# One fixed expert instead of two, its down projection at once, and expert weights in 16 KB rows

## The chip, the cores and the metric

The kernel runs on one core of one Trainium2 chip. The metric is the device time of one execution in microseconds (us). A time of the profiled execution is told beside the span that its profile covers, from the first to the last instruction. MB here is 2^20 bytes, as in the sizes of the transfers; GB/s are 10^9 bytes a second, as the profile prints them.

## The reference, cut to what matters

One decoder layer on 256 tokens of width 1024, all in float32. First a token mixer (layer norm, one wide input projection, two causal convolutions, gates, output projection), then a mixture of 32 experts, of which each token takes its four best:

```python
    logits = (xf @ router_w + router_b).astype(jnp.float32)
    top_v, top_i = lax.top_k(logits, TOP_K)          # TOP_K = 4 of 32
    gate = jax.nn.softmax(top_v, axis=-1).astype(u.dtype)
    ...
    def expert_block(args):
        xb, e = args
        h = clamped_swiglu(xb @ w1[e] + b1[e])       # w1[e]: 1024 x 2048
        return h @ w2[e] + b2[e]                     # w2[e]: 1024 x 1024
    ...
    y = jax.ops.segment_sum(ys * row_w[:, None], row_tok, num_segments=n_tok)
```

An expert has 8 MB of w1 and 4 MB of w2, so 384 MB of weights go through the second half. The routing of the reference, evaluated on its inputs, gives the experts between 0 and 136 tokens each; expert 0 has 26, expert 1 none, and it is the only one with none.

## The kernel before

**Two halves.** The mixer streams its weights (w_in, w_pb, w_pa, w_o and the modulation weights ada_w) as 64 transfers of 1 MB through a pool of sixteen 1 MB buffers, `wpool`. The expert half streams 384 transfers of 1 MB. Every weight transfer is issued by SP, in program order.

**Experts.** Tokens are gathered per expert in units of 32 (`gather`, a product of three bf16 parts of the normalised tokens with a selection matrix), go through w1 (`up`, accumulating over eight k-tiles of 128 rows), are transposed and put through the activation (`copy_up` on ACT, `turn` on TensorE, `swiglu` on VectorE), and through w2 (`down`). Four units make a group, and `combine` multiplies their gated rows back to the tokens. `ROOM[e]` is the number of units that the program reserves for the e-th expert in its order.

**Order.** The first `FIXED` = 2 experts are number 0 and 1, whatever the routing. The other 30 are taken in an order worked out on the chip: `rank()` counts for each expert how many have more tokens, and `plan_` says which rank stands at which place of the order (a 5-unit place for the largest, the last place for the smallest). `ordered()` turns the ranks with two products into `oc`, the numbers and token counts of the experts in their order. SP reads `oc` into registers before it issues the loads of an expert.

**Loads.** `order` lists the chunks: the eight of w1 of expert e, then the four of w2 of expert e-1. A w1 chunk is 128 rows of 8 KB; a w2 chunk is 256 rows of 4 KB, two for each partition. A ring of 17 buffers (the sixteen of `wpool` and one more) holds them. The first 17 loads are issued without a condition; every later one is issued by `used(e, k)`, in the program's place where the chunk 17 earlier has had its last product:

```python
            t = wtile()
            nc.sync.dma_start(t.rearrange("p (k f) -> p k f", k=src.shape[1]), src, cond=None if always else tokens > 0)
```

So a load whose expert has no token moves nothing.

**The expert loop.** For each e: `up(e)`, the gather of expert e+2, `down(e-1)`, the activation of e, and `combine` for finished groups. Small steps are put between the k-tiles of the first two `up`s as hooks: for expert 0 `ordered`, `in_order` of the positions, `bias1`, the gather of expert 1 and `in_order` of the gates; for expert 1 `select_gates(0)`, `gain` (the output gate as a row) and `bias2` (the gated second bias, added to the residual).

**The branch.** After expert 29, `beyond()` tests whether any expert has more tokens than its room, and if so works those off in loops; with these inputs it has none. At the end of that branch SP waits for all transfers in flight (the eight semaphores of its queue) before it goes on, and ACT waits for SP.

Of the kernel before, what the change touches and what calls it, by code (L numbers as in the profile page):

```python
# [20 lines left out]
SEQ = 256  # L21
KT = D // 128
NT = SEQ // 128
NE = 32
# [9 lines left out]

WBUFS = 16
XBUFS = 1
RING = WBUFS + XBUFS
NUNIT = SEQ // 32
# [72 lines left out]
def mixer_moe_kernel(ctx, tc, x, cond, packed, ada_w, ada_g1, w_in, w_pa, w_pb, w_o, ln1, ln2, router_b, w1, b1, w2, b2, plan, out):  # L111
    nc = tc.nc
    ctx.enter_context(tc.manual_schedule())
    wpool = ctx.enter_context(tc.tile_pool(name="wpool", bufs=WBUFS))
    keep = ctx.enter_context(tc.tile_pool(name="keep", bufs=1))
    state = {"pools": [wpool] * WBUFS, "n": 0, "ring": None}

    def wtile():
        pools, n = state["pools"], state["n"]
        state["n"] += 1  # L120
        ring = state["ring"]
        if ring is not None and n >= len(pools):
            return ring[n % len(pools)]
        t = pools[n % len(pools)].tile([128, 2048], F32, name="wchunk")
        if ring is not None:
            ring.append(t)
        return t

# [130 lines left out]

    xstack = ctx.enter_context(ExitStack())  # L260
    with ExitStack() as p1:
# [365 lines left out]
        wstack.close()  # L627
        xpool = xstack.enter_context(tc.tile_pool(name="xpool", bufs=XBUFS, side="right", reuse_waits="tile"))
        late = p1.enter_context(tc.tile_pool(name="late", bufs=1, reuse_waits="tile"))
# [159 lines left out]
    with ExitStack() as p2:  # L789
        one = p2.enter_context(tc.tile_pool(name="one", bufs=1, reuse_waits="tile"))  # L790
        sm = p2.enter_context(tc.tile_pool(name="sm2", bufs=1, reuse_waits="tile"))
        psb = p2.enter_context(tc.tile_pool(name="psb", bufs=1, space=PSUM, reuse_waits="tile"))
        state["pools"] = [wpool] * (WBUFS - 4) + [xpool] * XBUFS + [wpool] * 4
        state["n"] = 0
        state["ring"] = []
        ph = [psb.tile([128, 512], F32, name=f"ph{i}") for i in range(5)]
# [55 lines left out]
        def locate(e):  # L852

            if e < FIXED:
                where[e] = e, value(counts[0:1, e:e + 1], SEQ, (ENG.SP,))
            elif e < NE:
                where[e] = tuple(value(oc[0:1, v, e:e + 1], (NE - 1, SEQ)[v], (ENG.SP,)) for v in range(2))

        def load(n):
            if n >= len(order):  # L860
                return
            e, k = order[n]
            always = n < RING
            if k == 0 and e >= FIXED:
                if e == FIXED:
                    locate(e)
                locate(e + 1)
            if not always and e not in where:
                locate(e)
            i, tokens = where[e] if not always else (e, None)  # L870
            if k < KT:
                src = w1[bass.ds(i, 1), k * 128:(k + 1) * 128, :].rearrange("a p f -> p a f")
            else:
                src = w2[bass.ds(i, 1), (k - KT) * 256:(k - KT + 1) * 256, :].rearrange("a (k p) f -> p (a k) f", p=128)
            t = wtile()
            nc.sync.dma_start(t.rearrange("p (k f) -> p k f", k=src.shape[1]), src, cond=None if always else tokens > 0)  # L876
            wt[e, k] = t

        def used(e, k):
# [46 lines left out]
        def up(e, hooks={}):  # L926
            xt = xt_of(e)
            for kt in range(KT):
                w = wt[e, kt]
# [34 lines left out]
        def down(e):  # L964
            ddg = ddg_of(e)
            for u in range(ROOM[e]):
                q = bank_of[e, u]
                y, yt_, ys, cm = py[q % 2], yt[q % 2], ys_[:, q // 4 % 2, :], cms[q // 4 % 2]
                r = slice(32 * (q % 4), 32 * (q % 4) + 32)
                turn_gates(y, r, ddg[:, :, u * SLOT:(u + 1) * SLOT])  # L970
                for kt in range(KT):
                    o = (kt % 2) * 1024
                    w = wt[e, KT + kt // 2]
                    down_mm(y, acts[:, u], kt, [w[:, o + g * 256:o + (g + 1) * 256] for g in range(4)])
# [8 lines left out]
        def combine(i, banks, add=True):  # L983
            for t in range(NT):
                for h in range(2):
                    b = banks[(2 * t + h) % len(banks)]
                    nc.tensor.matmul(b, cms[i % 2][:, t * 128:(t + 1) * 128], ys_[:, i % 2, h * 512:h * 512 + 512],  # L987
                                     start=True, stop=True)
# [52 lines left out]
        def bias2():  # L1041
            for h in range(2):
                for t in range(NT):
                    a = X[:, t, h * 512:(h + 1) * 512]
                    nc.tensor.matmul(py[t], gatesT[:, t, :], b2w[0:NE, h * 512:(h + 1) * 512], start=True, stop=True)
                    tmp = sm.tile([128, 512], F32, name="hb")
                    nc.vector.tensor_tensor(tmp, py[t], hss[h], op=ALU.mult)
                    nc.vector.scalar_tensor_tensor(a, a, ALPHA, tmp, op0=ALU.mult, op1=ALU.add)

        def gain():  # L1050
            ada2_out(spare, sm, 5, None, ms=ms5)
            for h in range(2):
                pb = px.rearrange("p (k c) -> p k c", k=4)
                for k in range(4):
                    c = 40 + 4 * h + k
                    nc.tensor.matmul(pb[:, k, :], modT[:, c:c + 1].to_broadcast([128, 128]), identf, start=True, stop=True)
                nc.scalar.copy(hss[h], px)
                for g in (2 * h, 2 * h + 1):
                    nc.vector.tensor_copy(g2g[32 * g:32 * g + 32, :], hss[h][32 * g:32 * g + 32, (g % 2) * 256:(g % 2) * 256 + 256])
# [10 lines left out]
        def one_beyond(j, u):  # L1070
# [16 lines left out]
            for kt in range(KT):  # L1087
                for g in range(4):
                    w = hss[g % 2]
                    nc.sync.dma_start(w[:, None, :], w1[bass.ds(e, 1), kt * 128:(kt + 1) * 128, g * 512:(g + 1) * 512]  # L1090
                                      .rearrange("a p f -> p a f"))
                    nc.tensor.matmul(p[32 * g:32 * g + 32, :], xt[:, kt], w, start=(kt == 0), stop=(kt == KT - 1),
# [6 lines left out]
            for kt in range(KT):  # L1099
                for h in range(2):  # L1100
                    w = hss[h]
                    nc.sync.dma_start(w[:, None, :], w2[bass.ds(e, 1), kt * 128:(kt + 1) * 128, h * 512:(h + 1) * 512]
                                      .rearrange("a p f -> p a f"))
                    for g in (2 * h, 2 * h + 1):
# [38 lines left out]

        def gather_1():
            for piece in gather(1, py[0]):
                piece()

        hooks = {0: {2: ordered,
                     3: lambda: in_order(posm, posT, posS, px),
                     4: bias1,  # L1150
                     5: gather_1,
                     6: lambda: in_order(gates, gatesT, gateS, px)},
                 1: {1: lambda: select_gates(0), 2: gain, 5: bias2}}
        n_combined = 0
        for e in range(NE):
            pieces = []
            up(e, hooks.get(e, {}))
            if e + 2 < NE:
                select(e + 2)
                pieces = gather(e + 2)  # L1160
            if e:
                select_gates(e)
# [4 lines left out]
            if e:  # L1167
                down(e - 1)
# [54 lines left out]


def _cols(v):
    return v.reshape(-1, 128).T
# [51 lines left out]
```

## Time and profile before

| what | value |
|---|---|
| three runs, median (lowest to highest) | 1321.57 us (1320.34 to 1322.01) |
| profiled execution, its own time | 1321.0 us |
| its span | 1319.3 us |
| PE busy | 1139.7 us (86% of the span), 11387 instructions |
| VectorE, ACT busy | 527.3 us (40%), 132.2 us (10%) |
| moved by DMA | 473.42 MB, mean 359 GB/s (10^6 bytes) |
| granted TensorE clock, mean | 0.933 |

A busy PE in this table includes matmuls that wait in the pipeline, so its 86% is not a measure of work. The span has a mixer part up to about 330 us, in which TensorE is busy throughout, a router part up to about 341 us, and the expert loop, which ends at about 1301 us; the rest is the last layer norm and the output.

### The profile page before, as it was taken

The page shows a single profiled execution, that of the slowest core. Times are in us where ns is not written, and L with a number is a line of the kernel's source. Part 1 is how long each engine was busy: PE and PEld are TensorE (multiplying, and loading weights), DVE is VectorE, ACT ScalarE, POOL GpSimd, SP SyncE. Part 2 cuts the span into 40 slices and gives each one's busy share as a digit, 9 for nine tenths or more (in the row PEclk, how much of TensorE's full clock was granted, in tenths as well). Part 3 has the DMA queues.
Part 4 walks back from the last instruction along what each step waited for, and adds up shares of the span by engine and source line. Part 5 has one row for each costly group of instructions (what it writes and reads, how often), then busy time and mean ns, then how long its engine had stood idle before and what let it go on. Part 6 is the DMA issues. An engine that isn't in the chain of part 4 may idle for free. (4 is left out here: it accounts for less than half of the span.)

```text
span 1319.3 us, 26597 instructions
## 1 busy us (share of the span) xinstructions
PE 1139.7 (86%) x11387; PEld 633.0 (48%) x11388; DVE 527.3 (40%) x1352; ACT 132.2 (10%) x288; POOL 16.8 (1%) x34
## 2 busy tenths in 40 slices
PE   5999999997899998999897899797979787786644
PEld 4888888886435433544442335333423333232211
DVE  2588753656445314441442233223322332322214
ACT  2110001102110001010100010000000000000001
POOL 0000000001000000000000000000000000000000
PEclk9999999998889998999898999998979899897777
DMA  9974644776749999999999999999999999999975
GB/s 375 421 300 156 259 153 137 285 298 243 271 181 366 416 416 416 417 415 417 416 415 416 416 416 416 416 417 416 417 416 416 416 415 412 416 416 413 413 313 204
DMA packets 82223, 473.42 MB, mean 359 GB/s; under 512 B 7633, under 2 KB 7665, under 8 KB 41106
## 3 DMA queue, kind: packets, MB, share of 16 engines
q1 hardware_dynamic: 81250, 469.03, 88.4%
q10 hardware_dynamic: 848, 2.62, 0.5%
q8 instruction: 91, 1.49, 0.5%
q14 instruction: 34, 0.28, 0.1%
HBM read 474.76 MB, written 1.05 MB: 361 GB/s over the span
## 5 line engine op out<-in xcount | busy, mean ns | idle before, releaser
L923 PE MATMUL ph<-wchunk,xt 128*32 128x512 f32 x2368 | 295.7, 642 | 45.6 <-DMA wchunk<-in_w_dram 37.9
L956 PE MATMUL py<-wchunk,acts 128*32 128x256 f32 x3584 | 242.3, 404 | 48.4 <-DMA wchunk<-in_w_dram 46.3
L582 PE MATMUL zps<-slot,wchunk 128*128 128x256 f32 x1024 | 222.3, 379 | 1.6 <-DVE slot L301 1.6
L582 PEld LDWEIGHTS zps<-slot,wchunk 128*128 128x128 f32 x1024 | 194.3, 190 | 28.9 <-DVE slot L301 1.8
L956 PEld LDWEIGHTS py<-wchunk,acts 128*32 128x32 f32 x3584 | 137.9, 115 | 125.1 <-DMA wchunk<-in_w_dram 65.8
L923 PEld LDWEIGHTS ph<-wchunk,xt 128*32 128x32 f32 x2368 | 71.5, 114 | 248.3 <-issue 146.6
L923 PE MATMUL ph<-wchunk,xtm 128*32 128x512 f32 x1216 | 131.5, 592 | 0.0
L904 DVE TENSOR_TENSOR xt<-px,modT 128x256 f32<-128x256 f32 (+1 forms) x26 | 13.4, 517 | 294.6 <-PE px L901 294.6
L977 DVE TENSOR_TENSOR yt<-py,g2g 128x256 f32<-128x256 f32 x56 | 23.8, 425 | 240.7 <-PE py L956 240.7
L316 DVE SCALAR_TENSOR_TENSOR slot<-slot,pk,slot 128x256 f32<-128x256 f32 x240 | 97.6, 480 | 2.1 <-ACT slot L312 2.1
L923 PEld LDWEIGHTS ph<-wchunk,xtm 128*32 128x32 f32 x1216 | 39.0, 110 | 90.6 <-issue 90.0
L1122 ACT COPY hs<-ph 128x512 f32<-128x512 f32 x56 | 32.7, 584 | 424.5 <-PE ph L923 391.0
L901 PEld LDWEIGHTS <-slot 128*128 128x128 bf16 x1824 | 53.6, 99 | 33.2 <-issue 33.2
L980 DVE COPY slot<-yt 32x256 f32<-32x256 f32 x224 | 63.8, 285 | 4.6
L940 PE MATMUL ph<-identf,hs 128*128 128x128 f32 x224 | 36.5, 301 | 20.8 <-ACT hs L1122 20.8
L978 ACT COPY cm<-py 32x256 f32<-32x256 f32 x56 | 20.3, 363 | 322.6 <-DVE yt L977 322.6
L987 PE MATMUL px<-slot,cm 128*128 128x512 f32 x52 | 30.9, 678 | 21.4 <-DVE slot L991 19.4
L946 DVE TENSOR_TENSOR hb<-ph,b1S 128x512 f32<-128x512 f32 x56 | 38.7, 691 | 14.8 <-PE ph L940 11.5
L940 PEld LDWEIGHTS ph<-identf,hs 128*128 128x128 f32 x224 | 26.1, 151 | 34.9 <-ACT hs L1122 23.4
L901 PE MATMUL px<-dd,slot 128*128 128x32 bf16 (+1 forms) x1248 | 38.8, 185 | 0.0
L949 ACT ACTIVATE sg<-hb 128x256 f32<-128x256 f32 x56 | 23.3, 416 | 110.8 <-DVE hb L947 110.8
L904 DVE TENSOR_TENSOR xtm<-px,modT 128x512 f32<-128x512 f32 (+1 forms) x11 | 6.8, 618 | 62.2 <-PE px L901 62.1
(245 smaller groups left out, 697.8 us busy)
## 6 DMA issues: line engine op xcount, KB each, us to landing
wchunk<-in_w_dram SPq DMA_DIRECT2D x384, 1024.0 KB, 19.9
wchunk<-in_w_in_dram SPq DMA_DIRECT2D x28, 1024.0 KB, 13.5
wchunk<-in_ada_w_dram SPq DMA_DIRECT2D x24, 1024.0 KB, 8.3
wchunk<-in_w_pb_dram SPq DMA_DIRECT2D x4, 1024.0 KB, 8.0
wchunk<-in_w_pa_dram SPq DMA_DIRECT2D x4, 1024.0 KB, 4.8
wchunk<-in_w_o_dram SPq DMA_DIRECT2D x4, 1024.0 KB, 5.0
slot<-in_x_dram SPq DMA_DIRECT2D x2, 512.0 KB
slot<-in_x_dram ACTq DMA_DIRECT2D x1, 1024.0 KB, 10.0
```

What stands on the lines that cost most here:

```text
L316: nc.vector.scalar_tensor_tensor(cv[:, b, :], ya[:, b, k:k + SEQ], par("conv_a_w", b * CONV_A + k), cv[:, b, :], op0=ALU.mult, op1=ALU.add)
L582: nc.tensor.matmul(ps, w[:, o:o + 128], rhs[:, kt, :], start=(kt == 0), stop=(kt == KT - 1))
L901: nc.tensor.matmul(pv[:, kt], npart[c][:, t, kt * 128:(kt + 1) * 128], dd[:, t], start=(t == 0 and c == 0), stop=(t == 1 and c == 2))
L923: nc.tensor.matmul(p[32 * g:32 * g + 32, :], x_, w[g], start=(kt == 0), stop=(kt == KT - 1), skip_group_check=True)
L940: nc.tensor.transpose(pt[:, f].rearrange("p g s -> p (g s)"), hs[:, f * 128:(f + 1) * 128], identf)
L946: nc.vector.tensor_tensor(hb, pt, b1v.to_broadcast([128, 4, 4, SLOT]), op=ALU.add)
L949: nc.scalar.activation(sg, glu, AF.Sigmoid, scale=SW_ALPHA)
L956: nc.tensor.matmul(y[32 * g:32 * g + 32, 0:256], act[:, kt % 4, kt // 4, :], w[g], start=(kt == 0), stop=(kt == KT - 1), skip_group_check= ...
L977: nc.vector.tensor_tensor(yt_, y[:, 0:256], g2g, op=ALU.mult)
L980: nc.vector.tensor_copy(ys[r, g * 256:(g + 1) * 256], yt_[32 * g:32 * g + 32, :])
L987: nc.tensor.matmul(b, cms[i % 2][:, t * 128:(t + 1) * 128], ys_[:, i % 2, h * 512:h * 512 + 512], start=True, stop=True)
L1122: nc.scalar.copy(hss[q % 2], ph[q % 5])
```

## The change

It does six things.

1. `FIXED` is 1: only expert 0 is fixed; expert 1 is ranked with the others. Expert 0 keeps room for two units, the added ranked place has one.
2. `ordered()` runs before the first product of `up(0)`, and `rank()` before the first gather. The six loads of expert 0 are issued ahead, all others after `oc` is known.
3. `down(0)` follows the activation of expert 0, ahead of `up(1)`; for the later experts `down(e-1)` stays where it was.
4. The host lays w1 out as four blocks and w2 as two blocks of 128 rows of 16 KB for each expert. A load is 2 MB; an expert has six. The ring has 8 buffers of 2 MB. In the mixer the same buffers are used in halves of 1 MB, so one comes free when both halves have.
5. The last expert's w2 is loaded in eight pieces of 512 KB.
6. `gain` moves into `up(0)`, `bias2` into `up(2)`; b2 is multiplied by the output gate once (32 rows), which takes four VectorE operations out of `bias2`; `combine` uses only the rows that the last group has.

```diff
-WBUFS = 16
-XBUFS = 1
-RING = WBUFS + XBUFS
+RING = 8
...
-FIXED = 2
-ROOM = [2, 2] + [int(c) for c in "121511241121412131213121212111"]
-_RANK_ROOM = [5, 4, 4, 3, 3] + [2] * 8 + [1] * 17
+FIXED = 1
+ROOM = [2] + [int(c) for c in "1121511241121412131213121212111"]
+_RANK_ROOM = [5, 4, 4, 3, 3] + [2] * 8 + [1] * 18
...
     def wtile():
...
+        if not halves_:
+            t = wpool.tile([128, 4096], F32, name="wchunk")
+            halves_.extend((t[:, 0:2048], t[:, 2048:4096]))
+        return halves_.pop(0)
...
         for e in range(NE):
-            order += [(e, k) for k in range(KT)]
-            if e:
-                order += [(e - 1, k) for k in range(KT, 12)]
-        order += [(NE - 1, k) for k in range(KT, 12)]
+            order += [(e, k) for k in range(4)]
+            if e == 0 or e > 1:
+                order += [(max(0, e - 1), k) for k in (4, 5)]
+        order += [(NE - 1, k) for k in (4, 5)]
...
-            always = n < RING
+            always = e < FIXED
...
-            t = wtile()
-            nc.sync.dma_start(t.rearrange("p (k f) -> p k f", k=src.shape[1]), src, cond=None if always else tokens > 0)
+            src = w1[bass.ds(i, 1), k:k + 1] if k < 4 else w2[bass.ds(i, 1), k - 4:k - 3]
+            src = src.rearrange("a b p f -> p (a b) f")
+            t = ring[n % RING]
+            step = 4096 if e < NE - 1 or k < 4 else 1024
+            for f in range(0, 4096, step):
+                nc.sync.dma_start(t[:, None, f:f + step], src[:, :, f:f + step], cond=None if n < RING else tokens > 0)
...
-                used(e, kt)
+                if kt % 2:
+                    used(e, kt // 2)
...
-                    if u == ROOM[e] - 1 and kt % 2:
-                        used(e, KT + kt // 2)
+                    if u == ROOM[e] - 1 and kt % 4 == 3:
+                        used(e, 4 + kt // 4)
...
-        for n in range(RING):
+        for n in range(6 * FIXED):
             load(n)
...
+        rank()
         for piece in gather(0):
             piece()
-        rank()
-        select(1)
+        ordered()
+        for n in range(6 * FIXED, RING):
+            load(n)
         softmax(sm)
...
-        hooks = {0: {2: ordered,
-                     3: lambda: in_order(posm, posT, posS, px),
-                     4: bias1,
-                     5: gather_1,
-                     6: lambda: in_order(gates, gatesT, gateS, px)},
-                 1: {1: lambda: select_gates(0), 2: gain, 5: bias2}}
+        hooks = {0: {0: lambda: in_order(posm, posT, posS, px),
+                     2: bias1,
+                     3: lambda: in_order(gates, gatesT, gateS, px),
+                     4: gather_1,
+                     6: gain},
+                 2: {3: bias2}}
...
-            if e:
+            if e > 1:
                 down(e - 1)
...
+            if e == 0:
+                down(0)
...
-        "w1": a["w1"][0],
+        "w1": _rows(a["w1"][0], 2),
...
-        "w2": a["w2"][0],
+        "w2": _rows(a["w2"][0], 4),
```

How the instructions move is seen at three places. First the loads on SP around the reading of `oc` (TENSOR_LOAD); each conditional load is an ISA instruction and a DMA. Before:

```order
L876 DMA wchunk<-in_w_dram 128x2048 x16
L876 DMA wchunk<-in_w_dram 128x2x1024
L1136 DMA slot_96<-in_b_dram 32x2048
L1137 DMA xtm<-in_b_dram 32x1024
L849 TENSOR_LOAD counts
L876 ISA
L876 DMA wchunk<-in_w_dram 128x2x1024
L876 ISA
L876 DMA wchunk<-in_w_dram 128x2x1024
L876 ISA
L876 DMA wchunk<-in_w_dram 128x2x1024
L849 TENSOR_LOAD oc x4
```

And of the change:

```order
L861 DMA wchunk<-in_w_dram 128x4096 x6
L1130 DMA slot_96<-in_b_dram 32x2048
L1131 DMA xtm<-in_b_dram 32x1024
L838 TENSOR_LOAD oc x4
L861 ISA
L861 DMA wchunk<-in_w_dram 128x4096
L861 ISA
L861 DMA wchunk<-in_w_dram 128x4096
```

Twenty loads of 1 MB stood ahead of the reading of `oc`; now six of 2 MB do, and everything behind them waits for `oc`.

Second, VectorE between the ranks (`kr`) and `oc`. Before, the softmax of the gates stands between them, and the two operations that finish the gathered tokens of expert 0 stand ahead of both:

```order
L1004 SCALAR_TENSOR_TENSOR kr<-plan__89,rk 32x32
L888 TENSOR_SCALAR dd_1993<-slot_id,posm 128x64 x2
L776 TENSOR_SCALAR dl<-lg,m_0_93 128x32
L776 TENSOR_SCALAR dl<-lg,m_1_94 128x32
L779 TENSOR_SCALAR dl<-esg 128x64
L780 TENSOR_TENSOR esg<-esg,sel 128x64
L781 RECIPROCAL dl<-dl 128x64
L782 TENSOR_TENSOR esg<-esg,dl 128x64
L784 TENSOR_REDUCE ssum<-esg 128x2
L785 RECIPROCAL ssum<-ssum 128x2
L786 TENSOR_TENSOR gates<-esg,ssum 128x64
L1010 CAST oc<-py_1986 128x64
```

And of the change:

```order
L996 SCALAR_TENSOR_TENSOR kr<-plan__89,rk 32x32
L895 TENSOR_TENSOR xt_1962<-px,modT 128x512
L895 TENSOR_TENSOR xt_1962<-xt_1962,modT 128x512
L1002 CAST oc<-py_1959 128x64
L1004 COPY tokens<-py_1959 1x32
```

`oc` now comes directly behind the gathered tokens.

Third, TensorE after `up(0)`. `ph` is the result of `up`, `py` that of `down`. Before, the transposes of expert 0 are followed by `up(1)` with its hooks, and `down(0)` comes after that:

```order
L940 MATMUL ph_1981<-identf,hs_1999 128x128 x4
L940 MATMUL ph_1982<-identf,hs_2000 128x128 x4
L923 MATMUL ph_1983<-wchunk,xt_1990 32x512 x4
L923 MATMUL ph_1984<-wchunk,xt_1990 32x512 x4
L923 MATMUL ph_1983<-wchunk,xt_1990 32x512 x4
L923 MATMUL ph_1984<-wchunk,xt_1990 32x512 x4
L923 MATMUL ph_1983<-wchunk,xt_1990 32x512 x4
L923 MATMUL ph_1984<-wchunk,xt_1990 32x512 x4
L247 MATMUL px<-identf,csr 128x128 x2
L1056 MATMUL px<-identf,modT 128x128 x8
```

And of the change:

```order
L932 MATMUL ph_1954<-identf,hs_1972 128x128 x4
L932 MATMUL ph_1955<-identf,hs_1973 128x128 x4
L953 MATMUL py_1959<-identf,ddg_1968 32x128 x2
L948 MATMUL py_1959<-wchunk,acts 32x256 x32
L953 MATMUL py_1960<-identf,ddg_1968 32x128 x2
L948 MATMUL py_1960<-wchunk,acts 32x256 x32
L914 MATMUL ph_1956<-wchunk,xt_1963 32x512 x32
```

`down(0)` (L948) now stands between the transposes and `up(1)`.

## Rows read from the trace of the kernel before

**Rows 1.** Busy time, granted clock, DMA share and GB/s by stretch, expert loop and its end

```profile
404.00:1250.00 846.00, 731.51 (x8636) 322.38 (x8632) 275.44 (x748) 68.78 (x153) 0.00 (x0) 0.93 1.02 416
1250.00:1256.00 6.00, 6.00 (x95) 3.20 (x84) 0.00 (x0) 0.00 (x0) 0.00 (x0) 1.00 0.98 401
1256.00:1267.00 11.00, 0.50 (x8) 0.01 (x1) 1.56 (x5) 0.00 (x0) 0.00 (x0) 0.62 0.51 211
1267.00:1272.00 5.00, 3.50 (x16) 1.31 (x20) 2.10 (x6) 1.37 (x3) 0.00 (x0) 0.50 0.60 215
```

**Rows 2.** Order of time: what ACT does first after the branch

```profile
1267.86 0.59 ACT L1122 COPY hs<-ph 128x512 f32<-128x512 f32 x1 [33.45 <-SPq L1064]
```

**Rows 3.** DMA queue (packets, MB of 10^6 bytes, share) and issues (count, KB, us to landing)

```profile
q1 hardware_dynamic: 81250, 469.03, 88.4%
...
wchunk<-in_w_dram SPq DMA_DIRECT2D x384, 1024.0 KB, 19.9
...
wchunk<-in_w_o_dram SPq DMA_DIRECT2D x4, 1024.0 KB, 5.0
```

**Rows 4.** One source line, L876: instructions of SP, ns min/median/max

```profile
L876 SPq DMA_DIRECT2D wchunk<-in_w_dram x384: 73/383/4334, 264.3 to 1279.9; - x192
```

**Rows 5.** By stretch, as rows 1: between the last early loads and the loop

```profile
379.00:392.00 13.00, 12.60 (x60) 3.01 (x52) 6.31 (x12) 0.59 (x1) 0.00 (x0) 0.74 0.00 1
```

**Rows 6.** By stretch: only w2 moves (4 KB rows)

```profile
451.00:458.00 7.00, 7.00 (x124) 3.66 (x116) 2.55 (x9) 0.59 (x1) 0.00 (x0) 1.00 1.03 408
480.00:487.00 7.00, 7.00 (x72) 2.11 (x68) 0.00 (x0) 0.00 (x0) 0.00 (x0) 1.00 1.03 410
```

**Rows 7.** By stretch: only w1 moves (8 KB rows)

```profile
461.00:477.00 16.00, 16.00 (x188) 6.50 (x184) 6.01 (x19) 1.14 (x3) 0.00 (x0) 1.00 1.01 419
491.00:507.00 16.00, 15.79 (x215) 7.12 (x204) 1.97 (x6) 1.89 (x4) 0.00 (x0) 1.00 1.02 421
```

**Rows 8.** Order of time: gathered tokens, oc, and the loads that read it

```profile
340.50 0.69 DVE L904 TENSOR_TENSOR xt<-xt,modT 128x512 f32<-128x512 f32 x1
...
347.19 0.23 DVE L1010 CAST oc<-py 128x64 int32<-128x64 f32 x1 [2.05 <-PE py L1009]
...
349.07 15.79 SPq L876 DMA_DIRECT2D wchunk<-in_w_dram  x5
```

**Rows 9.** Order of time on TensorE: hooks and a two-unit up

```profile
348.94 0.39 PE L1025 MATMUL px<-identf,posm 128*32 128x128 f32 x2
...
350.40 1.92 PE L923 MATMUL ph<-wchunk,xt 128*32 128x512 f32 x16
...
352.25 3.75 PE L1037 MATMUL py<-kr,slot 32*128 32x32 f32 x32
...
371.91 0.44 PE L247 MATMUL px<-identf,csr 128*128 128x128 f32 x2
...
375.53 5.36 PE L923 MATMUL ph<-wchunk,xt 128*32 128x512 f32 x48
...
568.08 13.94 PE L923 MATMUL ph<-wchunk,xt 128*32 128x512 f32 x128
```

**Rows 10.** Order of time: end of up(0), its activations, down(0)

```profile
364.54 0.58 ACT L1122 COPY hs<-ph 128x512 f32<-128x512 f32 x1 [0.27 <-PE ph L923]
...
370.71 0.42 DVE L952 TENSOR_TENSOR acts<-hb,sg 128x256 f32<-128x256 f32 x1
...
393.71 0.52 PE L961 MATMUL py<-identf,ddg 128*32 128x128 f32 x3
...
401.42 1.09 PE L940 MATMUL ph<-identf,hs 128*128 128x128 f32 x8
```

**Rows 11.** Order of time: the last product with w2 of expert 30

```profile
1289.09 1.94 PE L956 MATMUL py<-wchunk,acts 128*32 128x256 f32 x16 [0.62 <-DMA wchunk<-in_w_dram]
```

**Rows 12.** Order of time on TensorE: up of experts 5 and 10

```profile
465.92 34.54 PE L923 MATMUL ph<-wchunk,xtm 128*32 128x512 f32 x320
...
638.28 8.27 PE L923 MATMUL ph<-wchunk,xt 128*32 128x512 f32 x64
```

More of the change, by code (lines that the diff above doesn't have):

```diff
@@ L113, in mixer_moe_kernel @@
     ctx.enter_context(tc.manual_schedule())
-    wpool = ctx.enter_context(tc.tile_pool(name="wpool", bufs=WBUFS))
+    wpool = ctx.enter_context(tc.tile_pool(name="wpool", bufs=RING))
     keep = ctx.enter_context(tc.tile_pool(name="keep", bufs=1))
-    state = {"pools": [wpool] * WBUFS, "n": 0, "ring": None}
+    halves_ = []
     def wtile():
[L119 to L127, printed above, removed]
+        if not halves_:
+            t = wpool.tile([128, 4096], F32, name="wchunk")
+            halves_.extend((t[:, 0:2048], t[:, 2048:4096]))
+        return halves_.pop(0)
     def wload(src):
@@ L792, in mixer_moe_kernel @@
         psb = p2.enter_context(tc.tile_pool(name="psb", bufs=1, space=PSUM, reuse_waits="tile"))
-        state["pools"] = [wpool] * (WBUFS - 4) + [xpool] * XBUFS + [wpool] * 4
-        state["n"] = 0
-        state["ring"] = []
+        ring = [wpool.tile([128, 4096], F32, name="wchunk") for _ in range(RING)]
         ph = [psb.tile([128, 512], F32, name=f"ph{i}") for i in range(5)]
@@ L852, in locate @@
         def locate(e):
-            if e < FIXED:
-                where[e] = e, value(counts[0:1, e:e + 1], SEQ, (ENG.SP,))
-            elif e < NE:
+            if e < NE:
                 where[e] = tuple(value(oc[0:1, v, e:e + 1], (NE - 1, SEQ)[v], (ENG.SP,)) for v in range(2))
@@ L862, in load @@
             e, k = order[n]
-            always = n < RING
-            if k == 0 and e >= FIXED:
+            always = e < FIXED
+            if k == 0 and not always:
                 if e == FIXED:
@@ L867, in load, with first, second @@
                 locate(e + 1)
-            if not always and e not in where:
-                locate(e)
             i, tokens = where[e] if not always else (e, None)
[L871 to L874, printed above, removed]
-            t = wtile()
-            nc.sync.dma_start(t.rearrange("p (k f) -> p k f", k=src.shape[1]), src, cond=None if always else tokens > 0)
+            src = w1[bass.ds(i, 1), k:k + 1] if k < 4 else w2[bass.ds(i, 1), k - 4:k - 3]
[4 more added lines that the diff above has]
+                nc.sync.dma_start(t[:, None, f:f + step], src[:, :, f:f + step], cond=None if n < RING else tokens > 0)
             wt[e, k] = t
+        def first(e, kt):
+            return wt[e, kt // 2][:, kt % 2 * 2048:kt % 2 * 2048 + 2048]
+        def second(e, kt):
+            return wt[e, 4 + kt // 4][:, kt % 4 * 1024:kt % 4 * 1024 + 1024]
         def used(e, k):
@@ L928, in up @@
             for kt in range(KT):
-                w = wt[e, kt]
+                w = first(e, kt)
                 for u in range(ROOM[e]):
@@ L971, in down @@
                 for kt in range(KT):
-                    o = (kt % 2) * 1024
-                    w = wt[e, KT + kt // 2]
-                    down_mm(y, acts[:, u], kt, [w[:, o + g * 256:o + (g + 1) * 256] for g in range(4)])
-                    if u == ROOM[e] - 1 and kt % 2:
-                        used(e, KT + kt // 2)
+                    w = second(e, kt)
+                    down_mm(y, acts[:, u], kt, [w[:, g * 256:(g + 1) * 256] for g in range(4)])
+                    if u == ROOM[e] - 1 and kt % 4 == 3:
+                        used(e, 4 + kt // 4)
                 nc.vector.tensor_tensor(yt_, y[:, 0:256], g2g, op=ALU.mult)
@@ L983, in combine @@
         def combine(i, banks, add=True):
+            r = slice(0, 32 * min(4, n_units - 4 * i))
             for t in range(NT):
@@ L1045, in bias2 @@
                     nc.tensor.matmul(py[t], gatesT[:, t, :], b2w[0:NE, h * 512:(h + 1) * 512], start=True, stop=True)
-                    tmp = sm.tile([128, 512], F32, name="hb")
-                    nc.vector.tensor_tensor(tmp, py[t], hss[h], op=ALU.mult)
-                    nc.vector.scalar_tensor_tensor(a, a, ALPHA, tmp, op0=ALU.mult, op1=ALU.add)
+                    nc.vector.scalar_tensor_tensor(a, a, ALPHA, py[t], op0=ALU.mult, op1=ALU.add)
         def gain():
@@ L1057, in gain @@
                 nc.scalar.copy(hss[h], px)
+                b = b2w[0:NE, h * 512:(h + 1) * 512]
+                nc.vector.tensor_tensor(b, b, hss[h][0:NE, :], op=ALU.mult)
                 for g in (2 * h, 2 * h + 1):
@@ L1089, in one_beyond @@
                     w = hss[g % 2]
[L1090 to L1091 removed]
+                    o = kt % 2 * 2048 + g * 512
+                    nc.sync.dma_start(w[:, None, :], w1[bass.ds(e, 1), kt // 2:kt // 2 + 1, :, o:o + 512]
+                                      .rearrange("a b p f -> p (a b) f"))
                     nc.tensor.matmul(p[32 * g:32 * g + 32, :], xt[:, kt], w, start=(kt == 0), stop=(kt == KT - 1),
@@ L1101, in one_beyond @@
                     w = hss[h]
-                    nc.sync.dma_start(w[:, None, :], w2[bass.ds(e, 1), kt * 128:(kt + 1) * 128, h * 512:(h + 1) * 512]
-                                      .rearrange("a p f -> p a f"))
+                    o = kt % 4 * 1024 + h * 512
+                    nc.sync.dma_start(w[:, None, :], w2[bass.ds(e, 1), kt // 4:kt // 4 + 1, :, o:o + 512]
+                                      .rearrange("a b p f -> p (a b) f"))
                     for g in (2 * h, 2 * h + 1):
@@ L1160, in mixer_moe_kernel @@
                 pieces = gather(e + 2)
-            if e:
-                select_gates(e)
+            select_gates(e)
             for u in range(min(2, ROOM[e])):
@@ L1222, in _chunks, with _rows @@
     return np.ascontiguousarray(w.reshape(KT, 128, n, cols).transpose(2, 1, 0, 3)).reshape(n, 128, KT * cols)
+def _rows(w, k):
+    n, m = w.shape[0], w.shape[2]
+    return w.reshape(n, -1, k, 128, m).transpose(0, 1, 3, 2, 4).reshape(n, -1, 128, k * m)
 def _cols(v):
```

6 lines of the change are left out of this document (2 added, 4 removed).

## The prediction

> **What bounds the kernel now.** I read the busy time by stretch first. From 404 to 1250 us DMA runs at 416 GB/s with a share of 1.02, so the 16 engines never rest [rows 1]; TensorE is "busy" 732 of those 846 us, but much of that is pipelined waiting. The expert loop is bound by its weight stream, so what counts is when the stream becomes continuous, how many MB it then has to move, at what rate, and what follows the last byte. At the end of the loop the share falls to 0.51 from 1256 to 1267 us: the engines do not end together, and the branch behind expert 29 drains the queue. ACT, which waits for SP there, goes on at 1267.86, after 33.45 us idle [rows 2]. So the stream covers 863.9 us from 404.0 to 1267.9. By the GB/s of rows 1 it moves 352.0 + 2.4 + 2.3 million bytes in it, 340 MB. By the list of loads 339 MB are weights: the branch stands behind the last use of w2 of expert 28, place 355 of the list; the load 17 places later is number 372, so 11 MB follow it; 4 MB are never moved (below); 30 MB came before 404. That is 2.548 us per MB.
>
> The queue shows what is not moved. The 384 expert transfers and the mixer's 64 are 448 MB, 469.8 million bytes without x, biases and output; the queue that carries all of these moved 469.03 [rows 3]. Expert 1 has no token; its w1 is loaded unconditionally, its w2 (4 MB) is not. This fits the stretch 379 to 392 us with 1 GB/s [rows 5]: the ring is full, the next four loads move nothing, and `down(0)`, which would free more, starts at 393.71 [rows 10].
>
> **Step 1, the start.** The six loads of expert 0 land long before `up(0)`, as before. `oc`: before, its CAST is at 347.19 and the first load that reads it goes out at 349.07, 1.65 us after the CAST's end [rows 8]. Now it follows the gathered tokens, which end at 341.2, so: CAST to 341.4, load at 343.1. A lone 1 MB transfer takes 5.0 us to land (w_o's four [rows 3]); less the 2.5 us that 1 MB takes, 2.5 us pass before data. The stream begins at 345.6. At 4.93 us for 2 MB (step 2) loads 6 to 11 run to 375.2 if their buffers are free in time. `up(0)` starts at 341.2; 16 k-tile units take 13.94 us, 1.74 per k-tile of two units; the hooks cost 1.5 (`in_order`, 348.94 to 350.40), 3.7 (`bias1`), 3.6 (`gain`, 371.91 to 375.53) [rows 9], and I take 1.4 each for the gates and the gather. Buffers come free at 346.2, 353.4, 359.7 and 366.8, each ahead of its need (355.5, 360.4, 365.4, 370.3 less 2.5). The next buffer waits for `down(0)`. Before, the activations of both units were ready 6.6 us after `up(0)` ended (364.5 to 371.1), the first 2.2 us earlier, and `down(0)` took 7.7 us [rows 10]. So: 366.8 + 4.4 + 3.8 + 1.9 = 377, data at 379.5, a gap of 4.3 us; then `up(1)`, whose weights are there, frees four more within 10 us. From 379.5 the stream has 24 MB behind it and does not stop. At 404 it has 33.8 MB, against 30: about 9 us won.
>
> **Step 2, the rate.** 4 KB rows move at 408 and 410 GB/s [rows 6], 8 KB rows at 419 and 421 [rows 7]: 2.564 and 2.497 us per MB; two to one they give 2.519, 416 GB/s, just rows 1. (2.548 holds 0.029 more, the uneven end.) Halving the rows per MB from 256 to 128 saves 0.067 us; if each row costs the same, halving again saves 0.034. That gives 2.463 us per MB (426 GB/s), 0.056 under the mix, and 2.492 with the uneven end. No row of the trace has 16 KB, so the bounds: saving stops at 8 KB (2.526); rows do not matter (2.548); worse than 4 KB (a rival below). I take the line, since the mix shows it holding between the two lengths. The Trainium skill ("DMA: Bandwidth & Descriptors", Specifications) puts the smallest transfer at line rate at 512 B; by it all three lengths are equal, the rate stays, and the sum is 1303. The trace does not agree: 408 to 410 against 419 to 421 GB/s.
>
> **Step 3, the bytes.** Ranked last, expert 1 now stands at place 31, and all its loads are behind the ring's first eight, so conditional: 12 MB are not moved instead of 4. 372 MB move. The branch has expert 29 ahead as before; the load issued last before it is the eighth after place 177 (the last of expert 28's w2), number 185, already one of expert 31's. So 368 MB stand ahead of the drain and 4 MB (w2 of expert 30) behind it. 344 MB x 2.492 = 857.2 us; from 379.5 the drain ends at 1236.7.
>
> **Step 4, the end.** Before, 215 GB/s in the 5 us after 1267 [rows 1] are 2.6 us of full rate, so data came at 1269.4, 1.5 us after the release. Now two empty loads go out first, at about 0.4 us each by the median issue; an empty one may cost only 0.07 [rows 4]: data at 1236.7 + 2.3. Before, seven chunks (three of w1, four of w2: 17.8 us at rate) were all in by 1289.09 [rows 11], 1.9 us over. Now 4 x 2.463 + 1.9 = 11.8: 1250.8. From that product on the kernel took 30.2 us to 1319.3. Now a transfer holds four k-tiles of w2 instead of two, one more such row of 1.9 us behind the landing; `down(31)` no longer waits for its last chunk (under 1 us): 30.9. `up(31)` fits into the 14 us in which w2 of expert 30 is fetched. The eight pieces of expert 31's w2 move nothing, so they give and take nothing.
>
> **Sum.** 1250.8 + 30.9 = 1281.7 us of span, against 1319.3; with the 1.7 us outside it 1283.4, against the profiled 1321.0. The median lies 0.6 above that execution: **1284 us**. About 9 us come from the start, 17 to 19 from the rate, the rest from bytes less a longer end.
>
> What costs nothing: the four VectorE operations fewer in `bias2`, the two added, the unit fewer and the shorter last `combine` lie beside the stream; without that cover the unit would be worth some 14 us of TensorE. In the mixer buffers come free in pairs, so a load can be a chunk later; TensorE takes far longer over a chunk there than DMA, and has fifteen ahead of it.
>
> **The rivals.**
> - *16 KB rows gain nothing over 8 KB.* For it: nothing in the trace is that long. Against: the even step from 4 to 8. 344 x 0.034 = 12 more: 1296.
> - *Row length does not matter*, the mix being low for another reason. 344 x 0.056 = 19 more: 1303.
> - *TensorE becomes the bound* around experts 5 to 10. From `up` of 5 to `up` of 10 it took 172.4 us [rows 12]; the 60 MB that belong to these five experts take 153 us now and 149.5 after. The lag of 19 us grows to 23 and the ring shrinks from 17 MB in 1 MB steps to 16 in 2 MB steps, about 43 to 39 us of stream. If less than 7 us of room are left, the stream stops for the difference: 1284 to 1291.
> - *Expert 1's loads are not dropped*: 4 MB more before the drain, 8 behind it, 30 us, less 11 for a shorter end and 0.8 for the empty issues: 1302.
> - *Slower.* 16 KB rows move worse than any shorter ones, because the 16 engines, each on a few long rows of one 2 MB block, hinder each other. The place is the whole loop. It decides from 406 GB/s down: 40 us (to 0.2% over 1321.6) over 344 MB are 0.117 per MB, 2.580. At 400 GB/s (2.621) the time is 1338. Against it: the rate rises with the row, and 406 lies under the 4 KB rows.
> - *The engines end more evenly*, with half as many transfers to wait for: up to 10 us less (344 x 0.029), 1274.
>
> **How the numbers follow.** Forecast 0.50, 8 KB as good 0.17, row length without effect 0.10, TensorE 0.10, loads not dropped 0.03, even end 0.05, slower 0.05. The likeliest is 1284. The range goes from the even end to no effect of rows, 1273 to 1304. A measurement of this kernel tells about 0.2% from no change. All cases but one are faster by more: faster 0.93, same 0.02, slower 0.05.
>
> **What would show it.** The stretch between 404 and 1200 us at 424 to 428 GB/s; a first load that reads `oc` at 343; an idle queue from about 322 to 345, a gap of some 4 us near 377, and none after that; `down(0)` at 371 to 379; the queue's MB down by 8.4 million bytes; ACT's first copy after the branch near 1237, and 45 us from there to the end. Wrong would be: 419 GB/s or less (step 2), stops between 460 and 700 us (TensorE), a later `down(0)` (step 1, each us counts), or a longer wait at the branch.

## The result and the profile after

The changed kernel takes **1284.22 us** (median of 4 runs, 1281.54 to 1288.37) against 1320.95 (4 runs, 1320.11 to 1322.01) in the same session: ratio 0.9724, 95% interval 0.9697 to 0.9752. Repeated unaltered it took 1284.40 us (5 runs, 1282.77 to 1286.60; before 1320.28), ratio 0.9728 (0.9713 to 0.9743). That second figure is the one beside which the experiments stand.

Two profiled executions of the same kernel are shown, since they differ by 4.1 us: the first with a span of 1286.6 us, the slowest of its four runs, the second with 1282.5. First, the changed kernel's first execution by stretch, with the columns of [rows 1]:

```profile
347.00:375.00 28.00, 25.56 (x264) 13.93 (x256) 6.77 (x22) 3.52 (x7) 0.00 (x0) 0.88 0.95 388
350.00:359.00 9.00, 8.55 (x50) 4.93 (x53) 0.04 (x1) 0.95 (x2) 0.00 (x0) 0.62 1.01 431
375.00:385.00 10.00, 9.03 (x151) 5.84 (x155) 5.75 (x17) 1.32 (x4) 0.00 (x0) 1.00 0.50 180
404.00:1200.00 796.00, 686.64 (x8276) 311.52 (x8268) 261.30 (x707) 65.86 (x146) 0.00 (x0) 0.95 1.01 426
460.00:700.00 240.00, 223.35 (x2731) 104.69 (x2724) 84.95 (x231) 21.92 (x50) 0.00 (x0) 0.98 1.00 425
1227.00:1239.00 12.00, 8.83 (x60) 2.65 (x64) 0.00 (x0) 0.00 (x0) 0.00 (x0) 0.72 0.54 224
```

The same view of the second execution:

```profile
347.00:375.00 28.00, 24.59 (x320) 14.76 (x323) 10.00 (x29) 4.13 (x8) 0.00 (x0) 1.00 0.94 398
350.00:359.00 9.00, 8.55 (x111) 3.82 (x114) 1.37 (x5) 0.95 (x2) 0.00 (x0) 1.00 1.01 433
375.00:385.00 10.00, 10.00 (x127) 5.78 (x116) 3.58 (x14) 0.73 (x2) 0.00 (x0) 1.00 0.73 280
404.00:1200.00 796.00, 681.95 (x8207) 307.65 (x8205) 260.06 (x705) 65.97 (x146) 0.00 (x0) 0.94 1.01 426
1224.00:1235.00 11.00, 10.37 (x87) 3.68 (x91) 0.00 (x0) 0.00 (x0) 0.00 (x0) 0.76 0.45 191
```

The loop moves 426 GB/s in both, where [rows 1] had 416. There is one gap, around 380 us, and none like it between 460 and 700; one slice of the first execution's page, some 32 us from 547, dips to 417 GB/s, which is under 1 us lost. The two executions part in two places. The table below has `oc`, which is ready before `up(0)` begins, 2.1 us earlier in the second. And in the stretch 350 to 359 the granted clock is 0.62 in the first (for part of it TensorE had the lower of its two levels, 1.2 GHz), 1.00 in the second. At the branch the engines still don't end together, a share of 0.54 over 12 us and of 0.45 over 11 us, as in [rows 1].

The bytes of the queue, on the page of the first execution, beside [rows 3]:

```profile
q1 hardware_dynamic: 37442, 460.62, 85.8%
```

469.03 less 460.62 is 8.41 million bytes: the 8 MB of expert 1 (8.39 million bytes) no longer move. Now the start in the second execution, SP's loads from 376 us and the work of TensorE ahead of them in order of time:

```profile
376.77 2.06 SPq L861 DMA_DIRECT2D wchunk<-in_w_dram  x2
```

```profile
339.89 1.92 PE L914 MATMUL ph<-wchunk,xt 128*32 128x512 f32 x16 [0.94 <-DVE xt L895]
...
346.77 3.75 PE L1029 MATMUL py<-kr,slot 32*128 32x32 f32 x32
350.45 1.92 PE L914 MATMUL ph<-wchunk,xt 128*32 128x512 f32 x16
...
370.90 3.66 PE L948 MATMUL py<-wchunk,acts 128*32 128x256 f32 x64 [1.62 <-DVE acts L944]
```

`up(0)` begins at 339.9 and `down(0)` at 370.9; load 12, the first whose buffer `down(0)` frees, goes out at 376.77. In the first execution it went at 381.85, 5.1 us later. Of these, 2.1 us were there at `oc`, and 2.8 lie in `bias1` (L1029) and the k-tile behind it, here in the first execution:

```profile
348.87 4.80 PE L1029 MATMUL py<-kr,slot 32*128 32x32 f32 x32
353.60 3.64 PE L914 MATMUL ph<-wchunk,xt 128*32 128x512 f32 x16
```

Last, the end in the second execution, ACT's first copy behind the branch, as [rows 2], and TensorE's last wait for a weight:

```profile
1235.03 0.59 ACT L1116 COPY hs<-ph 128x512 f32<-128x512 f32 x1 [19.03 <-SPq L1056]
```

```profile
1250.39 3.26 PE L948 MATMUL py<-wchunk,acts 128*32 128x256 f32 x32 [2.82 <-DMA wchunk<-in_w_dram]
```

Where the prediction gave a time, the two executions have:

| us | predicted | first | second |
|---|---|---|---|
| `oc` cast ends | 341.4 | 342.1 | 340.0 |
| first load that reads `oc` | 343.1 | 343.8 | 341.7 |
| load 12 issued | 377 | 381.9 | 376.8 |
| ACT goes on behind the branch | 1236.7 | 1240.3 | 1235.0 |
| last weights there | 1250.8 | 1255.7 | 1250.4 |
| span | 1281.7 | 1286.6 | 1282.5 |

### The profile page after: what moved, and what is told of

Its sections match the earlier page's. It is cut to its first block, busy times and chain, and to the rows that moved or that the text cites. A ratio compares the mean times of both kernels' runs of the same rounds, so it can differ in the third digit from the quotient of the medians.

```text
span 1286.6 us, 25561 instructions
## 1 busy us (share of the span) xinstructions
PE 1118.4 (87%) x11251; PEld 636.3 (49%) x11252; DVE 521.8 (41%) x1340; ACT 130.8 (10%) x285; POOL 16.8 (1%) x34
## 3 DMA queue, kind: packets, MB, share of 16 engines
q1 hardware_dynamic: 37442, 460.62, 85.8%
## 5 line engine op out<-in xcount | busy, mean ns | idle before, releaser
L914 PE MATMUL ph<-wchunk,xt 128*32 128x512 f32 x2304 | 284.8, 644 | 50.5 <-DMA wchunk<-in_w_dram 43.7
L948 PE MATMUL py<-wchunk,acts 128*32 128x256 f32 x3520 | 230.2, 399 | 40.2 <-DMA wchunk<-in_w_dram 35.8
L914 PEld LDWEIGHTS ph<-wchunk,xt 128*32 128x32 f32 x2304 | 74.9, 116 | 239.7 <-issue 169.3
L948 PEld LDWEIGHTS py<-wchunk,acts 128*32 128x32 f32 x3520 | 138.2, 114 | 106.6 <-DMA wchunk<-in_w_dram 43.6
L1116 ACT COPY hs<-ph 128x512 f32<-128x512 f32 x55 | 32.1, 584 | 412.8 <-PE ph L914 393.6
L932 PE MATMUL ph<-identf,hs 128*128 128x128 f32 x220 | 33.3, 285 | 9.1 <-ACT hs L1116 9.1
L932 PEld LDWEIGHTS ph<-identf,hs 128*128 128x128 f32 x220 | 23.5, 142 | 21.9 <-ACT hs L1116 11.2
```

What stands on the lines that cost most here:

```text
L914: nc.tensor.matmul(p[32 * g:32 * g + 32, :], x_, w[g], start=(kt == 0), stop=(kt == KT - 1), skip_group_check=True)
L932: nc.tensor.transpose(pt[:, f].rearrange("p g s -> p (g s)"), hs[:, f * 128:(f + 1) * 128], identf)
L948: nc.tensor.matmul(y[32 * g:32 * g + 32, 0:256], act[:, kt % 4, kt // 4, :], w[g], start=(kt == 0), stop=(kt == KT - 1), skip_group_check= ...
L1116: nc.scalar.copy(hss[q % 2], ph[q % 5])
```

## The experiments

Each kernel is the changed one with the edit shown. Each was measured beside the kernel before on the same chip; differences in us are those of its ratio and 0.9728, times 1321, and are uncertain by some 3 us (2.5 to 4). Since the two executions above differ by 4.1 us, a profile is compared with the one of them that has the same granted clock from 350 to 359 us (0.52 to 0.65 is "low", 1.00 "full"). What else differs between executions, such as the time of `oc`, stays in these comparisons.

**The rows, at the same 2 MB.** Two kernels leave order and size of the loads and change the layout in memory. `e1_old_rows` (the lines are shortened):

```diff
-            src = w1[...k:k + 1] if k < 4 else w2[...k - 4:k - 3]   # 16 KB rows
+            src = w1[..., k * 256:(k + 1) * 256, :] as "(k p) f -> p k f"       # 2 x 8 KB
+            src = w2[..., (k - 4) * 512:(k - 3) * 512, :] as "(k p) f -> p k f" # 4 x 4 KB
```

> The changed kernel with the rows of before: the same 2 MB loads in the same order, but a load of w1 is two 8 KB rows in each partition and one of w2 four 4 KB rows. Theory (the cost hangs on the row length): 344 MB before the branch at 2.548 us for each MB in place of 2.492, so 19 us more, 1303 us, and 415 to 417 GB/s from 404 to 1200. Rival (it is the 2 MB transfer that runs faster, not its rows): 1284 us and 426 GB/s.

`e2_8k_rows`, with `_rows(w1, 1)` and `_rows(w2, 2)`, two rows of 8 KB in each partition for every load:

> The changed kernel with 8 KB rows throughout: 2 MB loads, two 8 KB rows in each partition for both weights. Theory (each halving of the rows costs the same again, a price for each row): 2.526 us for each MB, 12 us more, 1296 us, about 420 GB/s from 404 to 1200. Rival (8 KB is enough): 1284 us, 426 GB/s. Rival (only the transfer's size counts): also 1284 us.

Old rows: 1304.52 us, ratio 0.9885 (0.9863 to 0.9906), 21 us more. 8 KB rows: 1300.67 us, ratio 0.9834 (0.9818 to 0.9851), 14 us more. Both profiled executions have the low clock, like the first one above; their spans are 1306.1 and 1299.1, so 19.5 and 12.5 us more than 1286.6. The loop by stretch, old rows, then 8 KB rows:

```profile
404.00:1200.00 796.00, 681.83 (x8176) 309.32 (x8176) 255.00 (x688) 64.59 (x143) 0.00 (x0) 0.94 1.02 416
```

```profile
404.00:1200.00 796.00, 681.06 (x8238) 310.36 (x8232) 260.63 (x704) 65.89 (x146) 0.00 (x0) 0.95 1.01 420
```

416, 420 and 426 GB/s for the three layouts: the rate hangs on the rows, not on the transfer's size (the 2 MB loads with old rows run as the 1 MB loads of [rows 1] did), and 8 KB is not yet enough. The rivals fall. The pages count 77122, 61250 and 37442 packets on the queue. From 4 to 8 KB for w2 and from 8 to 16 KB for both weights a row then costs about the same: the three rates over the 344 MB ahead of the branch are 8.3 and 12.1 us apart, for 917 and 1376 rows fewer on each of the 16 engines, so some 9 ns for each row (an estimate from rounded rates). The layouts also change where in memory a transfer's rows lie; no run here separates that from the number of rows.

**The bytes.** `e3_load_last` loads the expert at the last place whatever its count:

```diff
-                nc.sync.dma_start(..., cond=None if n < RING else tokens > 0)
+                nc.sync.dma_start(..., cond=None if n < RING or e == NE - 1 else tokens > 0)
```

> The changed kernel, but the expert at the last place (the one without a token) is loaded whatever its count: 12 MB more. Theory (the queue's bytes set the end): 4 MB more before the branch and 8 MB behind it, 30 us at 2.49 us for each MB, less what the end saves when the last piece is 512 KB in place of 2 MB (up to 8 us): 1306 to 1314 us. Rival (the last expert's loads are hidden behind TensorE's work there): 1284 to 1288 us.

1300.73 us, ratio 0.9855 (0.9840 to 0.9870): 17 us more, and 16.4 by the spans (1298.9 against 1282.5, both with the full clock). Neither range held it. TensorE's last wait for a weight:

```profile
1279.82 0.64 PE L948 MATMUL py<-wchunk,acts 128*32 128x256 f32 x8 [0.32 <-DMA wchunk<-in_w_dram]
```

The 12 MB put off the last weights from 1250.4 to 1279.8, 29.4 us, as the theory has it. What follows them shrank from 32.1 us to 19.1, by 13 and not "up to 8": behind the last 512 KB stand 8 products of `down(31)` instead of half of `down(30)`, the activations of 31 and all of `down(31)`. The bytes count in full; what the short last piece saves at the end was priced too low.

**The branch.** `e4_no_branch` deletes the call of `beyond()` behind expert 29:

```diff
-            if e == NE - 3:
-                beyond()
```

> The changed kernel without the branch for overflowing experts near the end (it leaves out the handling of experts with more tokens than they have room; there are none here). Theory (the drain at the branch costs its restart, but the uneven end of the engines stays, once): from 1225 to 1256 us 7.7 MB moved, which take 18 us at 426 GB/s, 13 us less, and about 6 us of that come back as the lagging half of the engines at the real end: 6 us less, 1278 us. Rival (the lag arises at the branch and is gone with it): 12 to 13 us less, 1271 us. Rival (TensorE is busy 14 of the 16 us behind the branch and bounds there): 0 to 2 us less.

1281.33 us, ratio 0.9699 (0.9686 to 0.9713), 4 us less; by the spans 7.3 (1279.3 against 1286.6, both low clock). TensorE near the end:

```profile
1239.85 1.93 PE L948 MATMUL py<-wchunk,acts 128*32 128x256 f32 x32 [1.37 <-DMA wchunk<-in_w_dram]
1241.72 0.66 PE L932 MATMUL ph<-identf,hs 128*128 128x128 f32 x4
1242.30 7.07 PE L914 MATMUL ph<-wchunk,xt 128*32 128x512 f32 x64
```

After 1239.85 it waits for no weight any more: without the drain the weights of expert 30 are there before `up(31)` is done, and TensorE sets the end. So the theory and the rival that TensorE bounds there each hold in part; the rival of 12 to 13 us less falls. Between 4 us by the medians and 7.3 by the spans the size stays open.

`e10_branch_late` moves that call to `e == NE - 1`, behind `activate(31)`:

> The changed kernel with the branch for overflowing experts moved from behind expert 29 to behind activate(31), after the last load. Theory (the drain costs nothing once no load follows it, but TensorE's 6.2 us at the branch now stand on the path to the end): 7.3 us less, as in the profile without the branch, and 6.2 us more, so 1283 us, 0 to 2 us less than the changed kernel. Rival (only the drain made the branch dear): 1280 to 1281 us, as without the branch. Rival (the branch waits for all engines at the end, and costs more there): 1286 us or more.

1281.41 us, ratio 0.9700 (0.9679 to 0.9722), 4 us less; by the spans 2.9 (1279.6 against 1282.5, full clock). TensorE behind the branch, in the changed kernel's first execution and here:

```profile
1230.17 9.64 PE L914 MATMUL ph<-wchunk,xt 128*32 128x512 f32 x64 [6.21 <-PEq L1056]
```

```profile
1254.56 0.39 PE L953 MATMUL py<-identf,ddg 128*32 128x128 f32 x1 [3.99 <-DVEq L1056]
```

It lost 3.99 us here, not 6.2; 7.3 less 4.0 is 3.3, near the 2.9 found. The drain is the dear part of the branch, and where nothing has to be loaded behind it, it is cheap.

**The start.** `e5_down0_late` runs expert 0's second products where they were before, behind `up(1)`:

```diff
-            if e > 1:
+            if e:
                 down(e - 1)
...
-            if e == 0:
-                down(0)
```

> The changed kernel with down(0) put back behind the products of up(1), as it was before; the loads stay in the new order of places, but each is issued when its buffer is used up, so loads 14 to 17 now go ahead of 12 and 13. Theory (what counts is when the next buffer comes free, not which expert is finished): up(1) frees one about 3 us before down(0) did (381.9 us in the profiled run), so 2 to 4 us less, 1280 to 1282 us. Rival (finishing expert 0 at once is what pays): 8 us more, 1292 us. Rival (the start is hidden): 1284 us.

1280.48 us, ratio 0.9689 (0.9676 to 0.9703), 5 us less: finishing expert 0 at once is not what pays. Its profiled execution was by far the slowest of its six (1287.05, the others 1277.79 to 1280.69), with the low clock:

```profile
375.00:385.00 10.00, 10.00 (x151) 4.96 (x147) 5.34 (x15) 1.42 (x3) 0.00 (x0) 1.00 1.00 400
```

```profile
547.00:580.00 33.00, 30.73 (x348) 13.07 (x350) 14.19 (x34) 1.78 (x4) 0.00 (x0) 1.00 0.97 404
```

The first load that waits for a buffer of expert 1 (number 14) goes at 376.11, where load 12 went at 381.85, and the gap is all but gone (400 GB/s against 180). But the stream stops around 560 us, between experts 5 and 10: 404 GB/s over 33 us are 1.8 us lost at 427. SP waits there up to 11.4 us for `up` to free a buffer; it does so in both executions of the changed kernel too, so it is the rate and not this wait that shows the stop. This is the rival "TensorE becomes the bound"; in the changed kernel it shows only as a trace, 417 GB/s in one slice of the first execution's page and 425, so none, in the second. That the earlier start brings it on is not shown: the same slice has 395 GB/s in `e8_four_first` below, whose stream is not ahead (up to 404 us it moved 261 GB/s on average, as in the first execution).

`e7_gain_late` takes `gain()` out of `up(0)`'s hooks and runs it behind the products of `down(0)`, ahead of their evictions:

```diff
-                     6: gain},
+                     },
...
-                down(0)
+                down(0, gain)
```

> The changed kernel with gain() taken out of up(0) and put between down(0)'s products and their evictions. Theory (TensorE's work until down(0) sets when load 12 goes): up(0) is 3.6 us shorter, load 12 goes 3.6 us sooner, 1280.6 us. Rival (the gap is not on the path): 1284 us. Rival (gain now delays the combine and expert 1's activations, and TensorE never makes it up): 1284 to 1288 us.

1279.75 us, ratio 0.9695 (0.9680 to 0.9709), 4 us less, as the theory has it. At the low clock load 12 goes at 376.18 instead of 381.85; 1.6 of these 5.7 us were there at the first load already.

`e9_both` puts `down(0)` behind `up(1)` and `gain()` into `up(1)`, behind its k-tile 3:

> The changed kernel with down(0) behind up(1) and gain() moved into up(1) behind its k-tile 3. Theory (with down(0) late the queue is no longer stopped near 380 us, so a still earlier free buffer buys nothing): as with down(0) late alone, 1279 to 1281 us. Rival (the two edits add): 1277 us.

1279.91 us, ratio 0.9689 (0.9676 to 0.9702). The edits do not add: 5 us less, as with `down(0)` late alone. In its profiled execution (full clock) the gap is shut, so a buffer that comes free still earlier buys nothing there:

```profile
347.00:375.00 28.00, 26.12 (x302) 13.55 (x302) 10.36 (x32) 4.13 (x8) 0.00 (x0) 1.00 1.01 427
375.00:385.00 10.00, 10.00 (x194) 7.43 (x187) 3.06 (x8) 0.95 (x2) 0.00 (x0) 1.00 1.01 429
```

`e8_four_first` has `down(0)` late as in `e5_down0_late` and restores the order of the loads too, so that four loads instead of six can go ahead of `oc` (with `4 * FIXED` for `6 * FIXED` where they are issued):

```diff
-            if e == 0 or e > 1:
-                order += [(max(0, e - 1), k) for k in (4, 5)]
+            if e:
+                order += [(e - 1, k) for k in (4, 5)]
```

> The changed kernel with the order of loads of before for the first expert: the two w2 loads of expert 0 come behind expert 1's w1 loads and down(0) behind up(1), so only 8 MB in place of 12 can go before the order is known. Theory (bytes behind oc): 4 MB more behind it, 10 us, less the gap near 377 us that is gone (4.3 us by the prediction, about 9 us in the profiled run): 1 to 6 us more, 1285 to 1290 us. Rival (the start is hidden behind TensorE): 1284 us or less. Rival (finishing at once is worth all of the start's 9 us): 1294 us.

1287.66 us, ratio 0.9754 (0.9740 to 0.9768), 3 us more; by the spans 1.7 (1284.2 against 1282.5, full clock). Against `e5_down0_late`, which differs in this order and number alone, it is 9 us slower: about what 4 MB more ahead of `oc` are worth, 10 us at 2.49 us per MB.

`e6_oc_late` computes the order behind k-tile 0 of `up(0)`:

```diff
-        ordered()
-        for n in range(6 * FIXED, RING):
-            load(n)
...
-        hooks = {0: {0: lambda: in_order(posm, posT, posS, px),
+        hooks = {0: {0: ordered_loads,
+                     1: lambda: in_order(posm, posT, posS, px),
```

> The changed kernel with the order of the experts computed behind k-tile 0 of up(0) in place of ahead of up(0), and loads 6 and 7 behind it: oc comes about 4 us later. Theory (the 12 MB of loads 6 to 11 have slack against down(0), which sets when load 12 may go): 0 to 1.5 us more, 1284 to 1286 us, and the gap near 380 us smaller by about 4 us. Rival (every us until oc is a us of the queue): 4 us more, 1288 us.

1286.60 us, ratio 0.9735 (0.9718 to 0.9751): 1 us more, uncertain by about 3, and no difference by the spans (1282.3 against 1282.5, full clock). The first load that reads `oc` went at 346.05 instead of 341.71 (1.7 of these 4.3 us were there when `up(0)` began, at 341.57 against 339.89), load 12 at 379.15 instead of 376.77. The 4.3 us did not come through; the slack is there, though 1.5 and 0 us cannot be told apart by this.

**The changed kernel once more**, `after_again`, for its spread:

> The changed kernel once more, unaltered, for a closer median beside which the experiments stand (its four runs spread over 1281.5 to 1288.4 us, those of before over 1320.1 to 1322.0). Theory (the start now waits for TensorE, whose granted clock in up(0) differs from run to run): again a spread of 4 us or more, median 1283 to 1285 us, and the issue of load 12 in its profiled run as much earlier than 381.8 us as the span is shorter than 1286.6. Rival (the first profiled run was merely odd at its end): load 12 at 381 to 382 us whatever the span.

1284.40 us, 1282.77 to 1286.60, a spread of 3.8 us. In the profiled run load 12 went 5.1 us earlier than in the first one, and the span was 4.1 us shorter, so the rival falls. Of the theory's cause, the clock in `up(0)`, the two traces show 3.0 of these 5.1 us; the other 2.1 were there at `oc`, before `up(0)`, and 1.3 of them before 302 us, in the mixer.

**Start and end together**, `e11_both_and_branch`: `e9_both` with the branch at `e == NE - 1`:

> The changed kernel with down(0) behind up(1), gain() in up(1), and the branch moved behind activate(31): the edits at the start and at the end together. Theory (start and end are apart, so they add): 4.5 us less from the start and 3 us less from the end by the medians, 1277 us. Rival (with the queue ahead, TensorE is late at the branch's place or near 550 us, and the end gives nothing more): 1280 us, as with the start's edits alone.

1276.23 us (5 runs, 1275.08 to 1279.28), ratio 0.9660 (0.9647 to 0.9673): 9 us less than the changed kernel, its 5 from the start and 4 from the end. They add, and this version beats both kernels.

## Why the prediction was right

The theory was that the weight stream sets the time: when it becomes continuous, its rate, its bytes, and what follows the last one. The rival was that the gain would lie elsewhere (in the transfers' size, or in finishing an expert at once), or be hidden behind TensorE.

- **Step 1, the start.** Right to 1 us in the second execution, load 12 at 376.8 for 377, but in part by luck: `oc` came 1.4 us earlier than forecast, and from it to load 12 it took 36.8 us for 35.6. In the first execution load 12 came 4.9 us late: 0.7 at `oc`, the same 1.2 behind it, and 3.0 by a clock that the step took as full. Both differences go some way to the new spread of 4 to 7 us, against 2 to 4 before. Up to 404 us the two moved 266 and 261 GB/s on average, the kernel before 256: 4.0 and 2.0 million bytes more, so about 10 and 5 us won, for 9 forecast. The runs add a correction to how the change reads: sending six loads instead of four ahead of `oc` is worth 9 us of the new start, but running `down(0)` ahead of `up(1)` by itself costs 5, since `up(1)` frees a buffer sooner.
- **Step 2, the rate.** The line through two row lengths gave 426 GB/s, and 426 it is. The two layouts confirm it from the other side: 420 for 8 KB (419 to 421 in [rows 7]) and 416 for the mix. The Trainium skill ("DMA: Bandwidth & Descriptors", Specifications) would have all three at line rate from 512 B on; the runs do not agree, 416, 420 and 426 GB/s for the same bytes in the same order. The layouts that the rivals at 1296 and 1303 speak of took 1300.7 and 1304.5 us, the first 4.7 us more than its rival's time. An equal price for each row, which the step assumed, fits the three rates.
- **Step 3, the bytes.** Right: 8.41 million fewer, and from load 12's data (issue and 2.5 us) to the release 855.8 us in the second execution, 855.9 in the first, for 857.2 predicted. Loading the empty expert again costs 17 us.
- **Step 4, the end.** 46.3 us from the release to the end in the first execution, 47.5 in the second, for 45. In both 1.3 us of the difference lie between the release and the last weights (15.4 us for 14.1); the rest, in the second, lies behind them, where the products of `down(31)` took 6.5 us, against 5.1 in the first. The rival of a more even end falls: the share at the branch is 0.54 and 0.45, where [rows 1] has 0.51.
- **TensorE as the bound** cost under 1 us in this kernel, but it is near: around 560 us it cost 1.8 us in `e5_down0_late`, and the dip is deepest in `e8_four_first`, whose stream is not ahead. What decides how deep it is stays open.
- **The sum** is better than its terms. In the second execution the stretch up to the release is 1.4 us short and the end 2.5 us long; in the first the start is 4.9 us late. That the median, 1284.22, lies within 0.3 us of the 1284 forecast is luck, with four runs spread over 7 us.

What stays open: the smaller changes (`bias2`, `combine`, the unit fewer) were not tested alone. The lag of half the engines' traffic at the branch (191 to 224 GB/s for 11 to 12 us in both executions) is in the kernel before as well, it is there with other row lengths and it is not made by the branch's drain alone; no run here shows what makes it. In how many executions the clock falls in `up(0)` is not known: it did in 7 of the 13 profiled ones of these kernels.

## What to carry to other kernels

Where a weight stream never rests, its time is a sum: what may be sent before a decision is known, the bytes, a price for each row, and the stops at drains; each term can be read from a row and tested alone. Lay weights out so that a partition's share of a transfer is one long row (here up to 16 KB), and look at what a late decision still allows to be sent rather than at which piece of work is finished first. When a start is moved earlier, find the next instruction that frees a buffer: it sets the time now, and its clock comes into the spread.

## What the runs showed of the hardware that was not expected

Longer rows go on paying past 8 KB, and by as much as the prediction's line had it: 416 (4 and 8 KB mixed), 420 (8 KB) and 426 GB/s (16 KB) for the same bytes in the same order, some 9 ns a row on each engine by the estimate above. What was not expected lies elsewhere. The granted clock of one stretch of one kernel, 350 to 359 us, was 0.62 in one execution and 1.00 in another, and the way from `oc` to load 12 took 3.0 us more with the lower one. And of the branch that is never taken, the drain of the queue is only one part: TensorE itself stood 6.2 us there with the stream running and 4.0 us behind its end.
